# Hybrid decoder layer: the weight sums of the last feed-forward part are made in that part, and the factors of the dilated attention are worked out later

## The chip, the cores and the metric

The kernel runs on one core of a Trainium2 chip. The time is device time in microseconds (us) of one execution; "the time before" is the median of three runs. TensorE multiplies matrices, VectorE and ScalarE work on tiles in on-chip memory, POOL (GpSimd) does too and also issues transfers, and SP (SyncE) issues most transfers. Each engine runs its own instructions in order and waits for others by semaphores. "Granted clock" is the TensorE clock that the throttle granted, as a share of full speed.

## The reference, cut to what matters

```python
def swiglu(x, w_gate, w_up, w_down):
    return (jax.nn.silu(x @ w_gate) * (x @ w_up)) @ w_down

def dilated_attention(q, k, v):            # three groups (window, dilation), 4 heads each
    ...
    w = jax.nn.softmax(jnp.stack(lses), axis=0)            # over the groups
    o = jnp.sum(w[..., None] * jnp.stack(outs), axis=0)
    ...
def token_mixer(h, ...):
    ...                                     # proj = h @ w_in, split into q, k, v, gates, merge
    y_nsa = o_nsa.reshape(B, S, Q_NSA) @ w_nsa_o
    y_dil = o_dil.reshape(B, S, DIL_OUT) @ w_dil_o
    y = jax.nn.sigmoid(g_a) * y_nsa + jax.nn.sigmoid(g_b) * y_dil
    return y @ w_mix_out

def reference(x, ...):
    h = rms_norm(x, ffn1_pre)
    x = x + 0.5 * rms_norm(swiglu(h, ffn1 weights), ffn1_post)
    h = rms_norm(x, mix_pre)
    x = x + rms_norm(token_mixer(h, ...), mix_post)
    h = rms_norm(x, ffn2_pre)
    x = x + 0.5 * rms_norm(swiglu(h, ffn2 weights), ffn2_post)
    return x
```

x is 512 x 1024 in float32, the feed-forward width is 2816, and w_in is 1024 x 5656 (of it 2304 columns are q, k and v of the dilated attention and 2048 the two merge gates).

## The kernel before, in words

**Three parts in a row.** The first feed-forward part runs to about 320 us, the mixer (sparse attention, called nsa, then the dilated attention, called dil, then the output products) to about 790, and the last feed-forward part to the end.

**A float32 product is three matmuls.** Every operand is split into a rounded value (the cast on ScalarE, L162: tiles `whi`, and `x_s` where a slot named x holds it) and what is left (a subtraction on VectorE, L163: tiles `wlo`, or `SP_s`). Three matmuls (L185, L186, L187) multiply hi by hi, hi by lo and lo by hi into a bank of PSUM (`pb_F`, `pb_S`, `pb_V`, `pb_T`). So a weight comes by a transfer into a tile `raw`, is cast and subtracted, and only then can TensorE use it.

**The feed-forward parts work in pairs.** A part computes gate, up and their product for eleven pairs of feature blocks; `sums(p)` ends pair p and stores the odd half with a transfer of SP (L437, `odram`). The down product then uses seven block products, as in Strassen's method, and four of these need sums of blocks of the down weights. The sums are held in DRAM, `tdram` (four of them, td[0] to td[3]). The first load of a stored sum (L354, `raw<-tdram`) stands behind the last pair.

**Who makes these sums.** In the first part `weight_sums` makes them behind its own pairs, with 110 transfers of 256 KB through tiles `PT_s`. For the last part `table_sums` makes them: 32 transfers on POOL's queue from DRAM to DRAM, of 768 KB (24 of them) or 512 KB (8), four copies `wd` to `td` for each group of feature blocks (b = 0, 3, 6, 9; steps 0 and 1), then additions on top, by transfers that accumulate (step 2, then 5 and 8, or 4 and 6 for b = 9; each adds to, or reads, what an earlier one has written).

**Where the sums stand.** `after(name, src)` is a hook: where the table `SUMS_AT` has that name, POOL makes a copy of one element per partition from `src` (the mark, L1810) and issues the transfers of the table behind it. So the transfers can't start before `src` is there, and whatever POOL has behind the hook waits too. Before, the hooks stand all through the mixer: `rows`, `keys`, `gates`, `m2` to `m15` in nsa, `keys0`, `turn0` to `turn11`, `scaled1`, `scaled3` in dil, and `out0` to `out7` in the output products.

**The dilated attention's factors.** Each of the three groups leaves its maxima and sums of exponentials in a tile (`dst_t`). For groups 1 and 2, whose rows stand in another order, these go through DRAM (`sdram`, back as `nat_t`). The factors come from the minimum `mn` of the groups, three differences and exponentials `fac`, the sum `z`, its reciprocal and three products; two of them go through DRAM again (`fdram`, back as `gf_t`). POOL then scales all 12 x 4 tiles of probabilities (slots `PT_s`, `x_s`, `CP_s`, `CB_s`, L1673), and TensorE transposes the scaled tiles (L1722) and multiplies them with V. V is projected by a loop over pairs of weight blocks, `k0` = 0, 2, 4, 6, each of which casts and subtracts its weights (`wsplit`) and multiplies into four banks that VectorE reads (`Q_s`).

**The output products.** The merge gates were stored in `gdram` during the earlier work and come back as tiles (`SP_s<-gdram`) for the sigmoid. The end of nsa has its own weights, `in_nsa_w_cv` among them.

Transfers of the weights are issued by SP, in program order; a scheduler orders the instructions of every engine along the order in which the code is written, and `issue_after` adds an order between two of them.

Of the kernel before, what the change touches and what calls it, by code (L numbers as in the profile page):

```python
# [16 lines left out]
AF = mybir.ActivationFunctionType  # L17
OP = mybir.AluOpType
# [3 lines left out]
P = 128  # L22
# [3 lines left out]
NT = S // P  # L26
# [9 lines left out]
PLAN = (1, 2, 2, 5, 2, 2, 3, 5, 2, 1, 2, 1)  # L36
LOTS = (0, 2, 1, 3)
BLOCKS = ("P1", "P2", "P6", "P5", "P7", "P3", "P4")
SUMS_AT = dict(rows=[(0, 0), (0, 1)], keys=[(0, 2)], gates=[(0, 5)], m2=[(0, 8)],
               m14=[(3, 0)], m15=[(3, 1)], keys0=[(3, 2)], turn0=[(3, 5)], turn2=[(3, 8)],  # L40
               turn11=[(6, 0), (6, 1)], scaled1=[(6, 2)], scaled3=[(6, 5)], out0=[(6, 8), (9, 0)], out1=[(9, 1)], out3=[(9, 2)],
               out5=[(9, 4)], out7=[(9, 6)])
SUMMED = dict(P5=0, P6=1, P3=2, P7=3)
NSA_UNITS = 6
PLAIN_UNITS = 8
# [38 lines left out]
class Layer:  # L84
# [275 lines left out]
    def ffn(self, gu, wd, td, post, finish, xsrc, aside=None, opened=None):  # L360
# [3 lines left out]
        nc = self.nc  # L364
# [63 lines left out]
        def sums(p, ev, od):  # L428

            h = slice(0, 256), slice(256, 512)  # L430
            x, y = self.slot(X_TAGS[p] if opened else "CB" if p < KEEP else "PT"), self.slot("ring")
            nc.vector.tensor_sub(x[:, h[0]], ev[:, h[1]], od[:, h[1]])
            nc.vector.tensor_sub(x[:, h[1]], ev[:, h[0]], ev[:, h[1]])
            nc.vector.tensor_sub(ev[:, h[1]], x[:, h[0]], ev[:, h[0]])
            nc.vector.tensor_add(y[:, 0:256], od[:, h[0]], ev[:, h[1]])
            with self.tc.issue_after(self.last_refill):
                nc.sync.dma_start(self.odram[p], od)  # L437
                if opened or p < KEEP:
                    nc.sync.dma_start(self.sxdram[p], x)
                else:  # L440
                    kept[p] = x
                nc.sync.dma_start(self.ydram[p // 2][:, h[p % 2]], y[:, 0:256])
            E.append(ev)
            if opened:
                sums_behind(ev[:, 0:1], p + 1)

        def split_even(p):
            if p < later:
# [4 lines left out]
        def sums_behind(src, n):  # L453
            mark = self.sbt("mark", [P, 1])
            behind = nc.gpsimd.tensor_copy(mark, src).ins
            with self.tc.issue_after(behind):
                for q in SUMS[n]:
                    weight_sums(q)
# [56 lines left out]
        for m in range(len(t4)):  # L515
            n = 4 // len(t4)
            c = slice(m * n, m * n + n), slice(256, 512)
# [95 lines left out]
        for i, (p, name) in enumerate(todo):  # L613
# [6 lines left out]
            if p == NP - 1 and name in ("P4", "P3"):  # L620
                k0 = 2 * len(first)
                r = self.blocks_of.pop(("B11", k0))
# [605 lines left out]
    def nsa(self, fillers, sums):  # L1228
        nc = self.nc
        ident = lambda v: v  # L1230
        pe = self.positions()
        r = self.wcols([(C_KC, 256)])
# [13 lines left out]
            self.proj_T(None, b, (2 * P, S), w)  # L1246
        self.positions_T(pe)
        rows = [self.block_rows(b) for b, _ in early[:2]]
        self.after('rows', rows[1][1][:, 0:1])
        kw = early[3][0]  # L1250
        vw = self.v_weights()
        kparts = [self.k_parts(early[2][0], ident)]
        gs = [self.blocks(0, rows[0])]
        kparts.append(self.k_parts(kw, ident))
        self.after('keys', kparts[1][1][1][:, 0:1])
        gs.append(self.blocks(1, rows[1]))
        wq = self.wslots(self.wcols([(0, 64), (256, 64)]), ["Q", "Q", "of", "of"])
        self.v_nsa(vw)
        self.after('gates', self.gate[:, 3, 0:1])
        early = self.hidden_early(0)  # L1260
        self.oh, self.ol = [], []
        heads = [(i, half, br) for i in range(4) for half in range(2) for br in range(2)]
# [1 line left out]
        probs = {}  # L1264
        for n in range(len(heads) + LAG):
            if n < len(heads) and n % 4 == 0:
                i = n // 4
# [4 lines left out]
            m = n - LAG  # L1272
            if m >= 0:
                i, half, br = heads[m]
                with self.tc.issue_after(self.unit_mm) if m == 0 else ExitStack():
                    probs[m] = self.hb_probs(*live.pop(m), self.gate[:, :, (i + 4 * half) * 3 + 1 + br])
            if n < len(heads):
                i, half, br = heads[n]
# [6 lines left out]
            if m >= 0:  # L1285
                i, half, br = heads[m]
                with self.tc.issue_after(self.last_pool):
                    sums(m)
                if br == 0:
                    out = self.bank("V")  # L1290
# [196 lines left out]
    def dil(self, fillers, early_gates):  # L1487
        nc = self.nc
# [13 lines left out]
        stats, probs, raws, bias = [], [], {}, {}  # L1502
# [115 lines left out]
        pairs = {}  # L1618
# [4 lines left out]
        for j in range(2):  # L1623
            pairs[0, j] = project(0, j)
            self.load_blocks()
            self.after(f"keys{j}", pairs[0, j][0][1][:, 0:1])
            if j == 0:
                for name in ("T1", "T2", "T4", "T3"):
                    self.mix_token_sums((name,))
        for i, n in enumerate(PLAN):  # L1630
            (g, j), half = turns[i // 2], i % 2
            if (j, half) == (0, 0) and g:
                project(g, 0)
            attend(g, j, half)
            self.after(f"turn{i}", stats[g][:, 0, 2 * j + half, 0:1])
            blocks(n)

        nat = [stats[0]]
# [2 lines left out]
            nc.sync.dma_start(n_.rearrange("p t h s -> p t (h s)"), self.sdram[g].rearrange("(t p) c -> p t c", p=P))  # L1641
            nat.append(n_)
        mn = self.sbt("mn", [P, NT, 4])
        with self.tc.issue_after(self.last_sub):
            nc.vector.tensor_tensor(mn, nat[0][:, :, :, 0], nat[1][:, :, :, 0], op=OP.min)
        nc.vector.tensor_tensor(mn, mn, nat[2][:, :, :, 0], op=OP.min)
        fac = [self.sbt(f"fac{g}", [P, NT, 4]) for g in range(3)]
        z = self.sbt("z", [P, NT, 4])
        zt = self.sbt("zt", [P, NT, 4])
        for g in range(3):  # L1650
            nc.vector.tensor_sub(fac[g], mn, nat[g][:, :, :, 0])
            self.last_exp = nc.scalar.activation(fac[g], fac[g], AF.Exp).ins
            dst_ = z if g == 0 else zt
            nc.vector.scalar_tensor_tensor(dst_, nat[g][:, :, :, 1], 1e-30, fac[g], op0=OP.max, op1=OP.mult)
            if g:
                nc.vector.tensor_add(z, z, zt)
        nc.vector.reciprocal(z, z)
        gf = []
        for g in range(3):
            nc.vector.tensor_mul(fac[g], fac[g], z)  # L1660
            if g == 0:
                gf.append(fac[0])
            else:
                nc.sync.dma_start(self.fdram[g - 1].rearrange("(t p) c -> p t c", p=P), fac[g])
                f = self.sbt(f"gf{g}", [P, NT, 4])
                nc.sync.dma_start(f, self.fdram[g - 1].rearrange("(n r) c -> n r c", r=4))
                gf.append(f)

        for hh in range(4):
            for g in range(3):  # L1670
                for t in range(NT):
                    pr = probs[g][hh][t]
                    scaled = nc.gpsimd.tensor_scalar(pr, pr, gf[g][:, t, hh:hh + 1], None, op0=OP.mult).ins  # L1673
            with self.tc.issue_after(scaled):
                self.after(f'scaled{hh}')

        vt = []
        vtags = ["Q"] * 4 + ["KA"] * 4 + ["V"] * 4
# [8 lines left out]
        r = self.wcols([(C_VD, 256)])  # L1687
        ws = [self.wsplit(r[:, 4 * u:4 * u + 4], [4, 256]) for u in range(2)]
        vt.append([])
        for t in range(NT):  # L1690
            b = self.bank("FFVS"[t])
            c = slice(t * P, (t + 1) * P)
# [8 lines left out]
        for k0 in range(0, KT, 2):  # L1701
            if k0 % 4 == 0:
                r = self.raw(wv[:, k0:k0 + 4], [4, S])
            w = self.wsplit(r[:, k0 % 4:k0 % 4 + 2], [2, S])
            for j in range(2):
                xs = [x[k0 + j].rearrange("p (n r) -> p r n", r=4) for x in (self.xh, self.xl)]
                for t in range(NT):
                    self.mm3(banks[t], xs[0][:, t], xs[1][:, t], w[0][:, j], w[1][:, j], k0 + j == 0, k0 + j == KT - 1)
# [68 lines left out]
        for n in range(len(items) + 1):  # L1777
            if n < len(items):
                hh, g = items[n]
# [6 lines left out]
            hh, g = items[n - 1]  # L1786
# [5 lines left out]
            j, half = hh // 2, hh % 2  # L1792
# [9 lines left out]
    def after(self, name, src=None):  # L1802

        if name not in SUMS_AT:
            return
# [8 lines left out]
    def mixer(self, post, finish, sums):  # L1814
        nc, a, tc = self.nc, self.a, self.tc
# [23 lines left out]
        def early_sums(m):  # L1839
            self.lot_sums(0, m)  # L1840
            self.lot_sums(1, m - 5)
            self.after(f"m{m}")

        self.sums = sums
        self.nsa(fill_half, early_sums)
# [1 line left out]
        gates = [[None, None] for _ in range(KT)]  # L1847
# [44 lines left out]
        for d in range(KT):  # L1892
            if d % 4 == 0:
                rd = self.raw(wd[d // 4], [2, 512])
                w_d = self.wsplit(rd, [2, 512])
            if d % 2 == 0 and d >= EARLY:
                w = first_weights(d)
            b1, b2 = self.bank(), self.bank()
            if d >= EARLY:
                c = slice((d % 2) * P, (d % 2 + 1) * P)  # L1900
                for k in range(4):
                    self.mm3(b1, w[0][:, k, c], w[1][:, k, c], self.oh[k], self.ol[k], k == 0, k == 3)
            c = slice((d % 4) * P, (d % 4 + 1) * P)
            for k in range(2):
                self.mm3(b2, w_d[0][:, k, c], w_d[1][:, k, c], self.dh[k], self.dl[k], k == 0, k == 1)
            load_gates(d + GATES_AHEAD)
            g1, g2 = gates[d]
            for i, b in ((0, b1), (1, b2)):
                if i or d >= EARLY:
                    times(d, i, b, behind[d > 1])  # L1910
            nc.vector.tensor_add(g1, g1, g2)
            self.after(f'out{d}', g1[:, 0:1])
            hi, lo = self.slot(ytags[2 * d], F32R), self.slot(ytags[2 * d + 1], F32R)
            self.split(hi, lo, g1)
            ys.append((hi, lo))
# [201 lines left out]
```

## Time and profile before

| | |
|---|---|
| median of three runs | 1126.52 us (1125.6 to 1128.25) |
| profiled execution | 1127.78 us, of it the span 1125.9 us, granted clock 0.991 in the mean |
| TensorE busy | 1094.8 us (97%), 7166 matmuls |
| VectorE busy | 913.4 us (81%) |
| ScalarE busy | 665.9 us (59%) |
| POOL busy | 251.2 us (22%) |
| transfers | 250.65 MB, 223 GB/s in the mean; on POOL's queue 68.69 MB |

The span is what the profile's stretches and waits are measured in; the execution's own time has 1.9 us around it. Busy shares are means over the whole span. A wait is shown as "engine tile line <- engine tile line": the instruction that waited, and the one that ended its wait.

### The profile page before, as it was taken

Reading aid. Unit: us, or ns where it says so; the run is one execution under the profiler, and the core shown is the slowest. Engines: PE = TensorE matmul, PEld = TensorE weight load, DVE = VectorE, ACT = ScalarE, POOL = GpSimd, SP = SyncE. Lnnn points to the kernel's source line nnn. Section 1 sums busy time; section 2 is a strip of 40 time slices with the busy share of each in tenths; the row PEclk is TensorE's granted clock in tenths of the full one; section 3 lists DMA queues with packets and bytes.
Section 4 is the critical chain, followed back from the end, with each engine's and each line's share of the span. In section 5 each row is a group of like instructions: output and inputs, shape, how many; then the busy total and the mean of one; then the engine's idle time right before and its main releaser. Section 6 shows DMA issues by size and latency. Waiting matters only on the chain.

```text
span 1125.9 us, 19348 instructions
## 1 busy us (share of the span) xinstructions
PE 1094.8 (97%) x7166; PEld 987.5 (88%) x7166; DVE 913.4 (81%) x1569; ACT 665.9 (59%) x1202; POOL 251.2 (22%) x340
## 2 busy tenths in 40 slices
PE   9999999999999899999999999979999999999997
PEld 7899999987889787777999988867989999998885
DVE  6889999988787778787987547856888999989575
ACT  7455555566565678675887536635435555557452
POOL 0444454300021146453100068110000000000001
PEclk9999999999999999999999999989999999999999
DMA  9899999999864988866675747796324444479852
GB/s 353 240 277 327 303 283 297 286 338 329 281 201 156 278 278 235 236 166 200 157 224 180 263 126 180 220 300 222 113 97 143 137 133 135 121 230 295 283 183 100
DMA packets 88798, 250.65 MB, mean 223 GB/s; under 512 B 13024, under 2 KB 18176, under 8 KB 85760
## 3 DMA queue, kind: packets, MB, share of 16 engines
q1 hardware_dynamic: 68208, 180.44, 47.0%
q0 software_dynamic: 20064, 68.69, 24.3%
q8 instruction: 56, 0.92, 0.3%
q14 instruction: 38, 0.31, 0.1%
q10 hardware_dynamic: 432, 0.30, 0.1%
HBM read 214.73 MB, written 74.50 MB: 257 GB/s over the span
## 4 chain that ended last, share of the span: by engine, by line
PE 67%; DVE 13%; ACT 7%; DMA 7%; issue 3%; POOL 3%; SPq 0%; DVEq 0%; POOLq 0%; ACTq 0%
PE pb_S L187 6%; PE pb_F L187 6%; PE pb_F L186 6%; PE pb_F L185 6%; PE pb_S L185 6%; PE pb_S L186 6%; PE pb_T L187 5%; PE pb_T L185 5%; PE pb_T L186 5%; DVE wlo L163 3%; PE pb_V L185 2%; PE pb_V L186 2%; PE pb_V L187 2%; ACT whi L162 2%; POOL PT_s L1673 2%
## 5 line engine op out<-in xcount | busy, mean ns | idle before, releaser
L163 DVE TENSOR_TENSOR wlo<-raw,whi 128x1024 fp32r<-128x1024 f32 (+2 forms) x222 | 262.3, 1187 | 92.8 <-ACT whi L162 88.6
L162 ACT CAST whi<-raw 128x1024 fp32r<-128x1024 f32 (+2 forms) x222 | 225.8, 1019 | 125.7 <-PE pb_F L187 20.4
L185 PE MATMUL pb_F<-xhl_t,whi 128*128 128x256 f32 (+1 forms) x320 | 106.2, 332 | 0.3 <-DVE KA_s L930 0.2
L187 PE MATMUL pb_F<-xhl_t,wlo 128*128 128x256 f32 (+1 forms) x320 | 105.1, 328 | 0.0
L186 PE MATMUL pb_F<-xhl_t,whi 128*128 128x256 f32 (+1 forms) x320 | 104.9, 328 | 0.0
L206 POOL TENSOR_TENSOR rs_t<-rs_t,mhalf_t 128x1 f32<-128x1 f32 x20 | 13.3, 666 | 403.8 <-DVE rs_t L202 403.8
L185 PE MATMUL pb_S<-xhl_t,whi 128*128 128x256 f32 (+1 forms) x280 | 83.3, 297 | 0.0
L186 PE MATMUL pb_S<-xhl_t,whi 128*128 128x256 f32 (+1 forms) x280 | 83.1, 297 | 0.0
L187 PE MATMUL pb_S<-xhl_t,wlo 128*128 128x256 f32 (+1 forms) x280 | 83.1, 297 | 0.0
L185 PEld LDWEIGHTS pb_F<-xhl_t,whi 128*128 128x128 f32 x320 | 60.3, 188 | 5.7 <-issue 0.8
L187 PEld LDWEIGHTS pb_F<-xhl_t,wlo 128*128 128x128 f32 x320 | 60.2, 188 | 4.9 <-DVE wlo L163 0.3
L186 PEld LDWEIGHTS pb_F<-xhl_t,whi 128*128 128x128 f32 x320 | 60.3, 188 | 4.4 <-issue 0.2
L1193 POOL TENSOR_SCALAR SP_s<-SP_s,st_t 128x384 f32<-128x384 f32 (+2 forms) x48 | 48.9, 1050 | 58.7 <-ACT whi L162 17.3
L185 PE MATMUL pb_T<-xhl_t,whi 128*128 128x256 f32 x216 | 59.9, 277 | 0.0
L186 PE MATMUL pb_T<-xhl_t,whi 128*128 128x256 f32 x216 | 59.9, 277 | 0.0
L187 PE MATMUL pb_T<-xhl_t,wlo 128*128 128x256 f32 x216 | 59.9, 277 | 0.0
L186 PEld LDWEIGHTS pb_S<-xhl_t,whi 128*128 128x128 f32 x280 | 52.6, 188 | 2.2
L185 PEld LDWEIGHTS pb_S<-xhl_t,whi 128*128 128x128 f32 x280 | 52.6, 188 | 2.2
L187 PEld LDWEIGHTS pb_S<-xhl_t,wlo 128*128 128x128 f32 x280 | 52.6, 188 | 2.2
L162 ACT CAST whi<-tmp_t 128x1024 fp32r<-128x1024 f32 x36 | 36.4, 1051 | 30.4 <-DVE tmp_t L538 23.5
L185 PE MATMUL pb_T<-SP_s,whi 128*128 128x256 f32 x176 | 49.2, 279 | 1.6 <-ACT ring_s L1470 1.4
L187 PE MATMUL pb_T<-SP_s,wlo 128*128 128x256 f32 x176 | 49.0, 278 | 0.2 <-DVE wlo L163 0.2
(931 smaller groups left out, 3731.6 us busy)
## 6 DMA issues: line engine op xcount, KB each, us to landing
raw<-in_gu_dram SPq DMA_DIRECT2D x64, 512.0 KB, 5.3
raw<-tdram SPq DMA_DIRECT2D x40, 512.0 KB, 5.3
PT_s<-in_d_dram POOLq DMA_DIRECT2D x66, 256.0 KB, 6.9
raw<-in_d_dram SPq DMA_DIRECT2D x30, 512.0 KB, 4.6
tdram<-in_d_dram POOLq DMA_DIRECT2D x18, 768.0 KB, 12.0
ldram<-in_w_in_dram POOLq DMA_DIRECT2D x12, 1024.0 KB, 11.2
tdram<-PT_s POOLq DMA_DIRECT2D x44, 256.0 KB, 5.7
raw<-in_w_in_dram SPq DMA_DIRECT2D x11, 1024.0 KB, 5.5
```

Of the source, the lines that this page charges most:

```text
L162: self.last_cast = self.nc.scalar.copy(dsthi, src).ins
L163: self.last_sub = self.nc.vector.tensor_sub(dstlo, src, dsthi.bitcast(F32)).ins
L185: mm(out, lhi, rhi, start=start, stop=False, skip_group_check=skip)
L186: mm(out, lhi, rlo, start=False, stop=False, skip_group_check=skip)
L187: self.last_mm = mm(out, llo, rhi, start=False, stop=stop, skip_group_check=skip).ins
L206: nc.gpsimd.tensor_tensor(out=r, in0=v, in1=self.mhalf, op=OP.pow)
L1193: self.last_pool = nc.gpsimd.tensor_scalar(pp, pp, st[:, 1, t:t + 1], None, op0=OP.mult).ins
L1673: scaled = nc.gpsimd.tensor_scalar(pr, pr, gf[g][:, t, hh:hh + 1], None, op0=OP.mult).ins
```

## The change

1. `SUMS_AT` has eight names, `pair0` to `pair7`, and the hooks with these names stand in `sums(p)` of the last feed-forward part. All 32 sum transfers are now issued behind its first eight pairs, and all hooks in the mixer are gone.
2. In dil, the work from `mn` to POOL's scaling is a function, `factors()`, called in V's loop behind the weights of `k0 == 2` rather than ahead of the loop. The four transfers by `fdram` go to POOL's queue instead of SP's.

```diff
-SUMS_AT = dict(rows=[(0, 0), (0, 1)], keys=[(0, 2)], gates=[(0, 5)], m2=[(0, 8)],
-               m14=[(3, 0)], m15=[(3, 1)], keys0=[(3, 2)], turn0=[(3, 5)], turn2=[(3, 8)],
-               turn11=[(6, 0), (6, 1)], scaled1=[(6, 2)], scaled3=[(6, 5)], out0=[(6, 8), (9, 0)], out1=[(9, 1)], out3=[(9, 2)],
-               out5=[(9, 4)], out7=[(9, 6)])
+SUMS_AT = dict(pair0=[(0, 0), (0, 1)], pair1=[(3, 0), (3, 1)], pair2=[(0, 2), (3, 2), (6, 0)],
+               pair3=[(0, 5), (3, 5), (6, 1), (9, 0)], pair4=[(0, 8), (6, 2), (9, 1)], pair5=[(3, 8), (6, 5), (9, 2)],
+               pair6=[(6, 8), (9, 4)], pair7=[(9, 6)])
...
             if opened:
                 sums_behind(ev[:, 0:1], p + 1)
+            else:
+                self.after(f'pair{p}', ev[:, 0:1])
...
-        self.after('rows', rows[1][1][:, 0:1])
...
-        mn = self.sbt("mn", [P, NT, 4])
-        with self.tc.issue_after(self.last_sub):
-            nc.vector.tensor_tensor(mn, nat[0][:, :, :, 0], nat[1][:, :, :, 0], op=OP.min)
...
+        def factors():
+            with self.tc.issue_after(self.last_sub):
+                nc.vector.tensor_tensor(mn, nat[0][:, :, :, 0], nat[1][:, :, :, 0], op=OP.min)
...
-                nc.sync.dma_start(self.fdram[g - 1].rearrange("(t p) c -> p t c", p=P), fac[g])
+                    nc.gpsimd.dma_start(self.fdram[g - 1].rearrange("(t p) c -> p t c", p=P), fac[g])
...
-                nc.sync.dma_start(f, self.fdram[g - 1].rearrange("(n r) c -> n r c", r=4))
+                    nc.gpsimd.dma_start(f, self.fdram[g - 1].rearrange("(n r) c -> n r c", r=4))
...
-                    scaled = nc.gpsimd.tensor_scalar(pr, pr, gf[g][:, t, hh:hh + 1], None, op0=OP.mult).ins
-            with self.tc.issue_after(scaled):
-                self.after(f'scaled{hh}')
...
             w = self.wsplit(r[:, k0 % 4:k0 % 4 + 2], [2, S])
+            if k0 == 2:
+                factors()
...
-            self.after(f'out{d}', g1[:, 0:1])
```

The other hooks (`keys`, `gates`, `m`, `keys0` and `keys1`, `turn`) are taken out in the same way. The numbers of the lines shift by one to three in the changed kernel.

**POOL at the start of nsa.** The names: `rs_t` the norm's statistics, `mark_t` the marks, `tdram_95` the stored sums, `in_d_dram` the down weights of the last part, `dm_s` and `SP_s` distances and softmax pieces, `ldram` the tiles of another queue of weights. Before:

```order
L206 TENSOR_TENSOR rs_t<-rs_t,mhalf_t 128x1
L1810 COPY mark_t<-SP_s 128x1
L1316 DMA tdram_95<-in_d_dram 128x1536 x4
L1810 COPY mark_t<-KA_s 128x1
L1318 DMA tdram_95<-in_d_dram 128x1536
L1319 DMA tdram_95<-in_d_dram 128x1536
L1810 COPY mark_t<-gate_t 128x1
L1321 DMA tdram_95<-tdram_95 128x1536
L1493 AFFINE_SELECT of_s<-dm_s 128x256
L1193 TENSOR_SCALAR SP_s<-SP_s,st_t 128x384
```

Now:

```order
L205 TENSOR_TENSOR rs_t<-rs_t,mhalf_t 128x1
L1491 AFFINE_SELECT of_s<-dm_s 128x256
L1194 TENSOR_SCALAR SP_s<-SP_s,st_t 128x384
L1194 TENSOR_SCALAR SP_s<-SP_s,st_t 128x128
L1194 TENSOR_SCALAR SP_s<-SP_s,st_t 128x256
```

The three marks and seven sum transfers of this place have gone; POOL goes from the norm to the mask and the softmax pieces.

**VectorE around the factors.** Rows L951 (L952) read the scores of the last turn of attention; `Q_s` are V's banks, `wlo` V's and other weights, `SP_s` the residuals of the x slots. Before:

```order
L951 ISA dst_t 128x1
L163 TENSOR_TENSOR wlo<-raw,whi 128x1024
L1684 TENSOR_TENSOR Q_s<-pb_F,Q_s 128x4x64
L1646 TENSOR_TENSOR mn_t<-mn_t,nat_t 128x16
L1651 TENSOR_TENSOR fac_t<-mn_t,dst_t 128x16
L1651 TENSOR_TENSOR fac_t<-mn_t,nat_t 128x16 x2
L1654 SCALAR_TENSOR_TENSOR z_t<-dst_t,fac_t 128x16
L1654 SCALAR_TENSOR_TENSOR zt_t<-nat_t,fac_t 128x16
L1656 TENSOR_TENSOR z_t<-z_t,zt_t 128x16
```

Now:

```order
L162 TENSOR_TENSOR wlo<-raw,whi 128x1024
L1680 TENSOR_TENSOR Q_s<-pb_F,Q_s 128x4x64 x2
L1680 TENSOR_TENSOR Q_s<-pb_V,Q_s 128x4x64
L162 TENSOR_TENSOR wlo<-raw,whi 128x1024
L1680 TENSOR_TENSOR Q_s<-pb_S,Q_s 128x4x64
L1642 TENSOR_TENSOR mn_t<-dst_t,nat_t 128x16
L162 TENSOR_TENSOR wlo<-raw,whi 128x1024
L1643 TENSOR_TENSOR mn_t<-mn_t,nat_t 128x16
L162 TENSOR_TENSOR SP_s<-x_s 128x512
L1648 TENSOR_TENSOR fac_t<-mn_t,dst_t 128x16
L1648 TENSOR_TENSOR fac_t<-mn_t,nat_t 128x16 x2
```

The factors stand behind all four banks of V's first two weight blocks and the weights of the next, and residuals of weights and of x slots stand between their pieces.

**POOL from the scaling to the last part.** The probabilities (`PT_s`, `x_s`, `CP_s`, `CB_s`) are scaled, then, before, the sums of the output products follow:

```order
L1673 TENSOR_SCALAR x_s<-x_s,gf_t 128x128 x5
L1673 TENSOR_SCALAR CP_s<-CP_s,gf_t 128x128 x4
L1673 TENSOR_SCALAR x_s<-x_s,gf_t 128x128 x3
L1673 TENSOR_SCALAR CP_s<-CP_s,gf_t 128x128 x4
L1318 DMA tdram_95<-in_d_dram 128x1536
L1319 DMA tdram_95<-in_d_dram 128x1536
L1673 TENSOR_SCALAR x_s<-x_s,gf_t 128x128 x4
L1673 TENSOR_SCALAR CP_s<-CP_s,gf_t 128x128 x8
L1673 TENSOR_SCALAR CB_s<-CB_s,gf_t 128x128 x4
L1321 DMA tdram_95<-tdram_95 128x1536
L1810 COPY mark_t<-KB_s 128x1
L1323 DMA tdram_95<-tdram_95 128x1536
```

Now:

```order
L1670 TENSOR_SCALAR PT_s<-PT_s,fac_t 128x128
L1661 DMA fdram<-fac_t 128x4x4 x2
L1670 TENSOR_SCALAR PT_s<-PT_s,fac_t 128x256 x3
L1670 TENSOR_SCALAR PT_s<-PT_s,fac_t 128x128
L1670 TENSOR_SCALAR PT_s<-PT_s,fac_t 128x256 x3
L1663 DMA gf_t<-fdram 128x16 x2
L1670 TENSOR_SCALAR PT_s<-PT_s,fac_t 128x128
L1670 TENSOR_SCALAR PT_s<-PT_s,fac_t 128x256 x3
L1670 TENSOR_SCALAR PT_s<-PT_s,fac_t 128x128
L1670 TENSOR_SCALAR PT_s<-PT_s,fac_t 128x256 x3
L1670 TENSOR_SCALAR x_s<-x_s,gf_t 128x128 x4
```

The sums are gone from between and behind the scaling, and the factors' transfers stand among its first pieces.

More of the change, by code (lines that the diff above doesn't have):

```diff
@@ L1254, in nsa @@
         kparts.append(self.k_parts(kw, ident))
-        self.after('keys', kparts[1][1][1][:, 0:1])
         gs.append(self.blocks(1, rows[1]))
@@ L1258, in nsa @@
         self.v_nsa(vw)
-        self.after('gates', self.gate[:, 3, 0:1])
         early = self.hidden_early(0)
@@ L1625, in dil @@
             self.load_blocks()
-            self.after(f"keys{j}", pairs[0, j][0][1][:, 0:1])
             if j == 0:
@@ L1634, in dil @@
             attend(g, j, half)
-            self.after(f"turn{i}", stats[g][:, 0, 2 * j + half, 0:1])
             blocks(n)
@@ L1643, in dil @@
         mn = self.sbt("mn", [P, NT, 4])
-        with self.tc.issue_after(self.last_sub):
-            nc.vector.tensor_tensor(mn, nat[0][:, :, :, 0], nat[1][:, :, :, 0], op=OP.min)
[L1646 to L1663, printed above, removed]
-                nc.sync.dma_start(self.fdram[g - 1].rearrange("(t p) c -> p t c", p=P), fac[g])
-                f = self.sbt(f"gf{g}", [P, NT, 4])
-                nc.sync.dma_start(f, self.fdram[g - 1].rearrange("(n r) c -> n r c", r=4))
-                gf.append(f)
-        for hh in range(4):
-            for g in range(3):
-                for t in range(NT):
-                    pr = probs[g][hh][t]
-                    scaled = nc.gpsimd.tensor_scalar(pr, pr, gf[g][:, t, hh:hh + 1], None, op0=OP.mult).ins
-            with self.tc.issue_after(scaled):
-                self.after(f'scaled{hh}')
+        def factors():
+            with self.tc.issue_after(self.last_sub):
+                nc.vector.tensor_tensor(mn, nat[0][:, :, :, 0], nat[1][:, :, :, 0], op=OP.min)
+            nc.vector.tensor_tensor(mn, mn, nat[2][:, :, :, 0], op=OP.min)
+            fac = [self.sbt(f"fac{g}", [P, NT, 4]) for g in range(3)]
+            z = self.sbt("z", [P, NT, 4])
+            zt = self.sbt("zt", [P, NT, 4])
+            for g in range(3):
+                nc.vector.tensor_sub(fac[g], mn, nat[g][:, :, :, 0])
+                self.last_exp = nc.scalar.activation(fac[g], fac[g], AF.Exp).ins
+                dst_ = z if g == 0 else zt
+                nc.vector.scalar_tensor_tensor(dst_, nat[g][:, :, :, 1], 1e-30, fac[g], op0=OP.max, op1=OP.mult)
+                if g:
+                    nc.vector.tensor_add(z, z, zt)
+            nc.vector.reciprocal(z, z)
+            gf = []
+            for g in range(3):
+                nc.vector.tensor_mul(fac[g], fac[g], z)
+                if g == 0:
+                    gf.append(fac[0])
+                else:
+                    nc.gpsimd.dma_start(self.fdram[g - 1].rearrange("(t p) c -> p t c", p=P), fac[g])
+                    f = self.sbt(f"gf{g}", [P, NT, 4])
+                    nc.gpsimd.dma_start(f, self.fdram[g - 1].rearrange("(n r) c -> n r c", r=4))
+                    gf.append(f)
+            for hh in range(4):
+                for g in range(3):
+                    for t in range(NT):
+                        pr = probs[g][hh][t]
+                        nc.gpsimd.tensor_scalar(pr, pr, gf[g][:, t, hh:hh + 1], None, op0=OP.mult)
@@ L1841, in early_sums @@
             self.lot_sums(1, m - 5)
-            self.after(f"m{m}")
         self.sums = sums
```

## The prediction

> **What bounds the kernel.** I read the page first (busy shares, the 40 slices), then the waits of TensorE by stretch, then the table by stretches, and last the chain of waits around each hole. The page:
>
> ```profile
> span 1125.9 us, 19348 instructions
> DMA  9899999999864988866675747796324444479852
> ```
>
> TensorE is busy 1094.8 us of this span, so only some 31 us are to be had, and the question is in which holes they lie and what ends them. Three waits of the mixer, the longest it has there, carry the case (line waiting, what ended it, us in total, times, longest):
>
> ```profile
> PE pb_V L1039 <- ACT x_s L162: 4.7, 1, 4.7
> PE pb_S L185 <- ACT whi L162: 1.4, 1, 1.4
> PE pb_S L186 <- DVE wlo L163: 1.2, 1, 1.2
> PE pb_S L187 <- DVE wlo L163: 6.3, 1, 6.3
> ```
>
> In the table by stretches the last three columns are granted clock, DMA share and GB/s:
>
> ```profile
> 386.00:392.00 6.00, 1.39 (x5) 1.22 (x6) 3.03 (x7) 5.28 (x13) 0.00 (x0) 0.81 0.84 251
> 392.00:398.00 6.00, 6.00 (x31) 5.69 (x30) 4.49 (x14) 4.32 (x14) 1.42 (x2) 0.62 0.66 187
> 655.00:660.00 5.00, 2.43 (x7) 1.73 (x7) 4.65 (x16) 3.54 (x9) 3.29 (x3) 0.94 0.10 3
> 660.00:665.00 5.00, 5.00 (x17) 4.35 (x17) 3.40 (x6) 2.71 (x4) 5.00 (x4) 0.72 0.43 108
> 736.00:740.00 4.00, 0.00 (x0) 0.00 (x0) 2.27 (x3) 1.27 (x3) 0.84 (x1) 0.74 1.04 405
> 740.00:744.00 4.00, 3.79 (x9) 3.01 (x10) 2.18 (x5) 2.48 (x4) 1.04 (x2) 0.50 1.04 251
> ```
>
> Each hole is paid twice: the idle time, and then a lower clock on the work behind it. The second price is 0.38 x 6 = 2.3 us behind hole A (386), 0.28 x 5 + 0.06 x 5 = 1.7 behind B (655) and 0.50 x 4 = 2.0 behind C (736). A costs 4.7 + 2.3 = 7.0, B 2.6 + 1.7 = 4.3, C 6.3 + 2.0 = 8.3: together 19.6 us. The chain shows that a transfer ends each:
>
> ```profile
> 376.45 10.25 DMA raw<-in_nsa_w_cv_dram
> 640.07 8.95 DMA sdram<-dst_t
> 649.08 5.30 DMA nat_t<-sdram
> 726.31 10.23 DMA SP_s<-gdram
> ```
>
> In the 40 slices those places stand at a DMA share of 0.7 to 0.9, while the last part's pairs (844 to 985) stand at 0.4: there is room where the sums go.
>
> **The change, part by part.** 1. *The 32 sum transfers leave the mixer.* 24 of 768 KB and 8 of 512 KB, 22 MB. In A, seven of them run while the load is under way; the same kinds of load have these medians, under contention and over all:
>
> ```profile
> tdram<-in_d_dram POOLq DMA_DIRECT2D x6, 768.0 KB, 12.7
> raw<-in_w_in_dram SPq DMA_DIRECT2D x11, 1024.0 KB, 5.5
> SP_s<-gdram SPq DMA_DIRECT2D x12, 256.0 KB, 5.4
> KB_s<-gdram SPq DMA_DIRECT2D x4, 256.0 KB, 4.9
> ```
>
> A: with 5.5 us the load issued at 376.45 lands at 382.0 instead of 386.7, 4.7 earlier. ScalarE's queue behind it (a cast, eight pieces of softmax, the cast TensorE waits for, 3.7 us in all) moves along, but it also has casts of its own that end at 382.2, so I take 4.3 of the idle 4.7:
>
> ```profile
> 381.02 1.14 ACT L162 CAST x_s<-raw 128x512 fp32r<-128x512 f32 x2 [2.41 <-PE pb_S L946]
> ```
>
> Of the clock price I take half, 1.2, since the weight casts behind stay in ScalarE's pace. Bounds: 0 (the load is slow for its own sake) and 7.0.
>
> C: with 4.9 us the load issued at 726.31 lands at 731.2, 5.3 earlier, and all behind it up to the weight residual that TensorE waits for moves along. Of the idle 6.3 us 1.0 stays. A pause that small cost no clock elsewhere (8.64 busy of 10 us, in one wait, at 1.00):
>
> ```profile
> 570.00:580.00 10.00, 8.64 (x74) 8.44 (x73) 8.33 (x19) 9.45 (x19) 0.12 (x1) 1.00 0.62 223
> ```
>
> So 5.3 + 2.0 = 7.3. Bounds 2 and 8.3: five sum transfers (2.75 MB) are issued from 724.5, but twelve gate tiles and two weight tiles remain.
>
> The Trainium skill (DMA: Bandwidth & Descriptors, Anatomy of one DMA) fits a transfer as about 2 us plus its bytes at 436 GB/s; by it A's 1 MB would take an estimated 4.4 us and C's 256 KB an estimated 2.6, and the sum would be about 1.5 us better. The medians above are longer, as transfers here always overlap others, so they stand.
>
> 2. *The factors.* VectorE stands still for 11.4 us, in its own order, for the statistics' way through DRAM, with the residuals of V behind it:
>
> ```profile
> 654.48 0.18 DVE L1646 TENSOR_TENSOR mn_t<-mn_t,nat_t 128x16 f32<-128x16 f32 x1 [11.40 <-DMA nat_t<-sdram]
> 656.72 19.84 POOL L1673 TENSOR_SCALAR PT_s<-PT_s,fac_t 128x128 f32<-128x128 f32 x16 [15.68 <-DVE fac_t L1660]
> 676.53 3.79 POOL L1673 TENSOR_SCALAR x_s<-x_s,gf_t 128x128 f32<-128x128 f32 x5
> 638.96 2.08 POOL L1316 DMA_DIRECT2D tdram<-in_d_dram  x4 [0.29 <-issue]
> 684.04 0.44 PE pb_T L1722 x4
> ```
>
> Now the residuals of V's first two weight tiles stand ahead, so B goes whole: 4.3 us. But VectorE reaches the factors only behind the fourth V bank (about 650) and a residual, and three more residuals are mixed in (0.7 us each): last factor at about 656.5, where it was. The earlier landing (three 768 KB copies no longer beside it) thus buys nothing, and POOL starts its scaling at the same 656.7. POOL now also issues the factors' four transfers, taken from SP: 2.08 / 4 = 0.52 us each, 2.1 us before the group-1 tiles (bounds 0 and 4.4, at the 1.1 of the slowest copy issue). Their first four were ready at 676.53 + 3.79 x 4 / 5 = 679.6 and will be at 681.7. TensorE's transposes of them were at 684.04, could be at 679.7 and must now wait 2.0 us. So 4.3 - 2.0 = 2.3, less a new clock price of up to 1.7: I take 0.6, the lower end, as the two waits of B (2.6 us together) did cost clock. Bounds +4.3 and -1.7. SP loses four entries, which nothing waited behind.
>
> The Trainium skill (TensorE: Matmul & The Clock Gate, Why this matters for your kernels) asks only that idle gaps stay under about 3 us. By it a 2.0 us wait costs no clock and B gives 2.3, the sum 1.7 us better; B's rows, 0.72 behind 2.6 us of idle in two pieces, do not bear it out, so the lower end stays.
>
> 3. *The sums in the last part.* Its pairs must carry 22 MB more. The first part is the model: it makes the same sums behind its pairs with 110 transfers of 256 KB (27.5 MB). One stretch of each (TensorE, its loads, VectorE, ScalarE, POOL, clock, DMA), and their weight loads (count, KB, median landing):
>
> ```profile
> 110.00:120.00 10.00, 10.00 (x91) 10.00 (x90) 10.00 (x17) 5.82 (x9) 4.32 (x6) 1.00 1.01 260
> 900.00:910.00 10.00, 10.00 (x91) 10.00 (x90) 9.81 (x15) 6.80 (x9) 0.00 (x0) 1.00 0.48 128
> raw<-in_gu_dram SPq DMA_DIRECT2D x13, 512.0 KB, 6.0
> raw<-in_gu_dram SPq DMA_DIRECT2D x15, 512.0 KB, 3.9
> 113.95 0.50 SPq L437 DMA_DIRECT2D odram<-W_s  x1
> 132.99 0.49 SPq L437 DMA_DIRECT2D odram<-W_s  x1
> 901.49 0.43 SPq L437 DMA_DIRECT2D odram<-W_s  x1
> 920.53 0.42 SPq L437 DMA_DIRECT2D odram<-W_s  x1
> ```
>
> A pair takes 19.04 us in both, at DMA shares 1.01 and 0.48, and TensorE issues 91 matmuls in 10 us in both. So the sums cost nothing there; the cover is the ring of eight weight blocks, two pairs deep, so that a load has some 25 us where it needs 6. Bounds 0 and 2 us. The dates hold too:
>
> ```profile
> 958.62 0.43 SPq L437 DMA_DIRECT2D odram<-W_s  x1
> 1012.36 1.75 SPq L354 DMA_DIRECT2D raw<-tdram  x2
> ```
>
> The last sum is issued behind pair 7 (about 960) and lands some 13 us later; the first load of a sum is at 1012. Eight mark copies on POOL cost nothing: it has no other work between the norms and the end.
>
> *Sum:* A 4.3 + 1.2, B 0.6, C 5.3 + 2.0, last part 0: 13.4 us. Span 1125.9 - 13.4 = 1112.5. The profiled execution took 1127.78 with 1.9 around its span: 1114.4. The median of the runs shown is 1126.52, 1.26 below it, so I predict 1126.5 - 13.4 = 1113.1.
>
> **The rivals.**
> *R1, POOL is in time:* its scaling goes faster once VectorE is less busy beside it, and B keeps its 4.3. For: five tiles took 6.78 us at first and 5.89 later:
>
> ```profile
> 656.72 6.78 POOL PT_s L1673 x5
> 663.84 5.89 POOL PT_s L1673 x5
> ```
>
> Against: the four issues. 13.4 + 3.7 = 17.1, so 1109.4.
> *R2, the loads stay slow:* in A, three 1 MB weight loads are themselves under way at 376, in C twelve gate tiles and two weight tiles. The shares around A stay near 1.0 for 25 us, and half of it is SP's own 5.1 MB against 5.5 MB of POOL's. Half of A and C: 13.4 - 6.4 = 7.0, so 1119.5.
> *R3, slower: POOL falls behind the pairs.* Its queue is in order, and a sum waits for the landing of the copy under it. Pairs 2 to 6 hold two dependent landings each; at 13 us that is 26 us in a 19-us pair, 7 us lost per pair, 35 by pair 6. The mark copy that reads a pair's result then holds a ring tile, three of them, which VectorE needs two pairs on. It decides once a mark is over 19 us late; by 35 - 19 = 16 us, paid in full and with clock 2.0 behind it: 1113.1 + 18 = 1131. For: in the first part POOL was already some 10 us behind its pair (result stored at 113.95, mark at 123.73):
>
> ```profile
> 123.73 0.55 POOL L455 COPY mark_t<-KB_s 128x1 f32<-128x1 f32 x1
> ```
>
> Against: there it stayed 10 behind for eight pairs, and here the copy under a sum is one pair older.
> *R4, POOL is kept from issuing while VectorE works.* With only VectorE's idle 0.2 us of 10 (900 to 910), six issues of 0.52 us could not be made in a pair, the sums would still be under way at 1012, and every late us would stand on the path: 1140 or more. Against: at 110 to 120 VectorE is busy 10.00 and POOL issues all the same (4.32 us). The Trainium skill (SBUF — State Buffer, the 'DVE blocks DMA' trap) has this rule, for VectorE instructions that take both ports; the trace does not bear it out for the subtractions here.
> *R5, no change:* each hole reopens at the next late engine; 1126.5.
>
> **How the numbers follow.** Forecast 0.58, R1 0.14, R2 0.16, R3 0.05, R4 0.02, R5 0.05. A measurement of this kernel tells about 0.2% (2.3 us) from no change. Faster: 0.58 + 0.14 + 0.16 = 0.88; same 0.05; slower 0.07. The range reaches over R1's 1109.4, with B and C at their better ends, to 1108.0, and over R2's 1119.5 to 1120.5; outside lie R3 to R5 (0.12) and the rims.
>
> **What would show it.** Right: the clock row at 1.00 through the stretches of A and C; the load behind 376 landing in under 7 us and the gate tile in under 6; VectorE's 11.4 us wait gone, but POOL's scaling starting where it did and TensorE's transposes waiting for POOL by 1 to 3 us; pairs of the last part at 19.0 us with a DMA share near 0.8 to 0.9. Wrong: pairs longer than 19.3 us or SP waiting for a sum at the first load (R3, R4), A or C with over 3 us idle (R2), no wait for POOL (R1).

## The result, and the profile after

The changed kernel takes 1114.53 us (median of four runs, 1113.68 to 1115.58) against 1126.06 before (four runs, 1123.16 to 1128.25). The ratio is 0.990 with a 95% interval of 0.9875 to 0.9924, clear of 1: it is faster by 11.5 us. 1113.1 was forecast. The profiled execution took 1113.99. Its page:

```profile
span 1112.2 us, 19346 instructions
...
PE   9999999999999999999999999999999989999997
DMA  9899999999863478863265623673589997468862
```

The slices of TensorE at holes A and C (8 and 7 before) are 9 now, and there is a new 8 in the 33rd slice, in the last part, where transfers now stand at 9. The longest waits of TensorE between 320 and 800 us, then the only long one behind 800:

```profile
PE pb_T L184 <- ACT ring_s L1468: 1.4, 1, 1.4
PE pb_S L186 <- DVE wlo L162: 1.1, 1, 1.1
```
```profile
PE pb_T L184 <- ACT V_s L577: 3.9, 1, 3.9
```

The waits of A, B and C are gone (the 1.4 for `ring_s` was there before). The stretches that answer to those of before (A, B, C), and the new hole D:

```profile
386.00:392.00 6.00, 5.90 (x36) 5.01 (x36) 5.87 (x19) 5.92 (x16) 1.62 (x2) 1.00 0.70 209
655.00:660.00 5.00, 5.00 (x23) 5.00 (x22) 1.02 (x1) 0.67 (x1) 4.98 (x7) 1.00 0.13 35
736.00:740.00 4.00, 4.00 (x19) 3.34 (x18) 3.10 (x5) 2.94 (x6) 0.00 (x0) 1.00 0.90 328
886.00:890.00 4.00, 3.22 (x29) 3.02 (x27) 3.13 (x5) 1.57 (x2) 0.00 (x0) 1.00 1.03 242
890.00:893.00 3.00, 0.00 (x0) 0.00 (x0) 0.38 (x2) 0.82 (x3) 0.00 (x0) 1.00 1.02 406
893.00:897.00 4.00, 3.88 (x21) 3.88 (x22) 3.01 (x4) 1.02 (x2) 3.78 (x5) 0.63 1.03 415
```

TensorE is busy at clock 1.00 where the three holes were; at 890 it has nothing to do, then a clock of 0.63.

TensorE's instructions stand in the same order in both kernels, so the start of one and the same matmul in both traces shows where time was won. "Ahead by" is how much earlier that matmul starts now, and "step" what has been won since the row above. Worked out from the traces' matmul rows (us):

```
matmul behind       before     after    ahead by    step
(first part)        273.82    273.17      0.65
hole A              396.51    388.62      7.89     A  +7.2
(turns of dil)      626.20    618.82      7.38        -0.5
hole B              662.70    650.44     12.27     B  +4.9
hole C              744.92    725.50     19.43     C  +7.2
(norms)             786.65    767.01     19.64        +0.2
hole D              911.00    897.23     13.77     D  -5.9
end                1119.37   1105.41     13.96        +0.2
```

The profiled executions differ by 13.8 us (1127.78 and 1113.99); the one of before lies 1.7 above its median, the one of the changed kernel 0.5 below. The steps are thus those of two single executions, and they add up to more than the 11.5 us between the medians.

What ends D is seen in the chain of waits, and in the rows of ScalarE and POOL:

```profile
868.99 23.11 DMA ydram<-ring_s
```
```profile
892.18 0.42 ACT L424 ACTIVATE ring_s<-V_s 128x256 f32<-128x256 f32 x1 [4.13 <-DMA ydram<-ring_s]
893.18 0.52 POOL L1808 COPY mark_t<-ring_s 128x1 f32<-128x1 f32 x1 [18.37 <-DVE ring_s L425]
```

A pair's result y is stored from a slot of the ring `ring` (three slots). One store of 128 KB took 23.11 us. ScalarE needed that slot for its next product and stood still for 4.13 us, and with it, in its queue, the copy that empties TensorE's bank (`V_s`). POOL was not late: it had waited 18.37 us for the mark's source.

### The profile page after: what moved, and what is told of

Same layout as the page of the kernel before. It is cut to its first block, busy times and chain, and to the rows that moved or that the text cites. A ratio compares the mean times of both kernels' runs of the same rounds, so it can differ in the third digit from the quotient of the medians.

```text
span 1112.2 us, 19346 instructions
## 1 busy us (share of the span) xinstructions
PE 1090.3 (98%) x7166; PEld 984.8 (89%) x7166; DVE 913.1 (82%) x1569; ACT 666.5 (60%) x1202; POOL 236.6 (21%) x340
## 5 line engine op out<-in xcount | busy, mean ns | idle before, releaser
L205 POOL TENSOR_TENSOR rs_t<-rs_t,mhalf_t 128x1 f32<-128x1 f32 x20 | 13.5, 673 | 306.2 <-DVE rs_t L201 306.2
```

The source lines that it names most:

```text
L205: nc.gpsimd.tensor_tensor(out=r, in0=v, in1=self.mhalf, op=OP.pow)
```

## The experiments

Each was run in turn with the kernel before on one chip, and ratios are to that: E1 to E4 on one chip, E5 to E8 on a second, E9 to E11 on a third.

**E1, the sums alone.**

```diff
-            if k0 == 2:
-                factors()          # and mn ... scaling inline ahead of V's loop, fdram and gf on SP, as before
```

> The changed kernel with the factors put back ahead of V's loop and their transfers back on SP; the sums stay in the last part. Theory 1 (hole B came from the three sum copies beside the statistics' way through DRAM, so moving the sums alone closes it): the statistics land about 10 us sooner on this clockwork, VectorE waits under 4 us for them, TensorE has no wait over 1 us at that place, time as the changed kernel, 1114.5 (1113 to 1116). Theory 2 (it is the later place of the factors that closes B): the hole is back with 4.9 us, 1119.4 (1118 to 1121).

1114.83 us against 1124.24, ratio 0.9913 (0.9899 to 0.9928). No wait of TensorE over 1.4 us is left in the mixer, and VectorE's wait for the statistics is short:

```profile
DVE mn_t L1642 <- DMA nat_t<-sdram: 3.0, 1, 3.0
```

Theory 1: without the copies beside them the statistics come in time. D is there, with 4.4 us.

**E2, the factors alone.** The kernel before with `factors()` at `k0 == 2` and its transfers on POOL; all sums and hooks of the mixer stay.

> The kernel before with the later factors and their transfers on POOL, all sums left in the mixer. Holes A and C must stay (7 us each) and the new hole of the last part at 890 must not be there. Theory 1 (the sums alone make B): VectorE still waits for the statistics until about 654 and the residuals behind them are late, 1125 to 1126. Theory 2 (the later place closes B by itself): 1126.1 - 4.9 = 1121.2 (1120 to 1122.5). If both this and the sums alone close B, the two parts cover the same hole and are not to be added.

1121.01 us, ratio 0.9967 (0.9955 to 0.998): 3.2 us less. The waits of TensorE between 360 and 760:

```profile
PE pb_S L187 <- DVE wlo L163: 6.8, 1, 6.8
PE pb_V L1039 <- ACT x_s L162: 5.5, 1, 5.5
```

A and C stay, B is closed (a step of 4.9 us in the matmuls' starts, between the rows at 626.20 and 662.70 of before), D is absent. Theory 1's form for this run is wrong: the later place closes B by itself too. The time lies in theory 2's range, but that was worked out from 1126.1; from this chip's 1124.24, 4.9 us less would be 1119.3, and the medians show 3.2.

**E3, the sums spread; and E4, slots of their own for y.** E3:

```diff
-SUMS_AT = dict(pair0=[(0, 0), (0, 1)], pair1=[(3, 0), (3, 1)], pair2=[(0, 2), (3, 2), (6, 0)], ...
+SUMS_AT = dict(pair0=[(0, 0), (0, 1)], pair1=[(0, 2), (3, 0)], pair2=[(3, 1), (0, 5)],
+               pair3=[(3, 2), (0, 8)], pair4=[(6, 0), (3, 5)], pair5=[(6, 1), (3, 8)],
+               pair6=[(6, 2), (9, 0)], pair7=[(9, 1), (6, 5)], pair8=[(9, 2), (6, 8)], pair9=[(9, 4), (9, 6)])
```

> The changed kernel with the same 32 sum transfers spread over ten pairs, three or four behind each, instead of 4, 4, 6, 6, 5, 4, 2, 1. Theory P (the new hole of 5.4 us at 890 comes from too many sum transfers in flight behind pairs 2 to 4, which stretch a store to 23 us): the wait of 3.9 us is gone, no store of the part takes over 12 us, 1114.5 - 5.4 = 1109.1 (1108 to 1111). Theory Q (22 MB in this part cost what they cost wherever they stand): 1114.5, with a wait of the same size at another pair.

E4:

```diff
-            ..., self.slot("ring")
+            ..., self.slot("ring" if opened else {4: "PT", 5: "CB"}.get(p, "ring"))
```

> The changed kernel with the y tiles of pairs 4 and 5 in slots of their own instead of the ring of three; all transfers as they are. Theory R (the hole at 890 is a ring slot held by the slow store of y, on which ScalarE's next product waits): the 3.9 us wait goes though the transfers stay as slow as 20 us, 1109 to 1110.5. Theory W (with landings of 20 us the weights of the pairs are late too): the wait only changes its name to a weight tile, 1113 to 1115.

E3: 1106.85 us, ratio 0.9842 (0.9827 to 0.9856). E4: 1110.41 us, ratio 0.9878 (0.9859 to 0.9897). The landings of the y stores (least, median, most), of the changed kernel, E3 and E4:

```profile
DMA to landing us min/median/max: 2.8/4.9/23.1
```
```profile
DMA to landing us min/median/max: 3.6/4.0/7.0
```
```profile
DMA to landing us min/median/max: 3.2/6.0/25.2
```

E4 leaves the stores as slow as they were, and the 3.9 us wait is gone: the slot was the link (theory R). E3 leaves the slots and takes the slowness: gone as well (P). E3 gains more than its range said (1108 to 1111), of which 1.8 us are this chip's faster kernel before (1124.24, not 1126.06). E4 stays 3.6 us behind E3; waits for weights that land late, theory W's, are 1.4 of these:

```profile
PE pb_F L186 <- DVE wlo L162: 0.9, 1, 0.9
PE pb_S L186 <- DVE wlo L162: 0.5, 1, 0.5
```

**E5, E6, E7: one hole's transfers each, in the kernel before.** E5 moves `rows`, `keys`, `gates` and `m2` to pairs 0 to 3; E6 issues the copies of `turn11` behind `turn6`; E7 moves `out0` to `out7` to pairs 0 to 4. E5 moves 4, 2, 1 and 1 transfers to its four pairs, and E7 nine (eight are counted in what was expected of it).

> The kernel before with only the sums of the first group (seven of their eight transfers are under way around 386) moved to pairs 0 to 3, two to four transfers in a pair. Theory 1 (hole A is the sum transfers beside the load of the last nsa weights): the load lands in under 6 us, A closes, 7.0 us less than before (6 to 8), B and C stay, and no new hole in the last part. Theory 2 (SP's own loads slow each other there, rival R2): half, 3 to 4 us less.

> The kernel before with only the four copies that stand beside the statistics' way through DRAM issued earlier, behind turn 6 instead of turn 11; factors as before. Theory 1 (these copies make hole B): the statistics' two transfers take under 7 us instead of 14, VectorE waits under 4 us, B closes, 4 to 5 us less than before. Theory 2 (B is VectorE's order, whatever the copies): no change within 1 us. A and C stay in both.

> The kernel before with only the eight sum transfers of the output products moved to pairs 0 to 4, one to three in a pair. Theory 1 (hole C is these transfers beside the merge gates' tiles): the gate tile lands in under 6 us, C closes, 7.0 us less than before (6 to 8), A and B stay. Theory 2 (the twelve gate tiles and two weight tiles slow each other, rival R2): half, 3 to 4 us less.

E5: 1119.58 against 1124.53, ratio 0.9957 (0.994 to 0.9974). The two loads issued between 374 and 378 (the nsa weights and a projection's weights), before and in E5:

```profile
DMA to landing us min/median/max: 10.3/12.4/14.6
```
```profile
DMA to landing us min/median/max: 5.4/6.0/6.6
```

A closes (6.7 us in the matmuls' starts, between those at 273.82 and 396.51 of before); C stays, as two waits of 2.6 and 3.8 us. The median says 5.0 us less, which lies between the ranges of the two theories; the load, 5.4 us in place of 10.3, is what speaks for theory 1.

E6: 1122.56, ratio 0.9976 (0.9967 to 0.9985): 2.0 us by the medians (2.7 by the ratio), in neither theory's range, though the matmuls' starts say 4.8 at B. The profiled execution of before is 3.3 above this chip's median, so its holes may be larger than most executions have; that was not settled. The mechanism is in the trace: VectorE's wait at the statistics, 11.40 before, and no wait of TensorE at that place:

```profile
DVE mn_t L1646 <- DMA nat_t<-sdram: 2.8, 1, 2.8
```

E7: 1118.06, ratio 0.9938 (0.9925 to 0.9951), 6.5 us less. The stretches of C:

```profile
736.00:740.00 4.00, 4.00 (x19) 3.27 (x18) 4.00 (x6) 0.77 (x1) 0.00 (x0) 1.00 0.95 297
740.00:744.00 4.00, 4.00 (x19) 3.30 (x18) 2.28 (x4) 1.94 (x4) 0.00 (x0) 1.00 1.04 359
```

The twelve gate tiles are still there; the slowest lands in 5.8 us, where it was 11.1 before (before, then E7):

```profile
DMA to landing us min/median/max: 3.3/5.4/11.1
```
```profile
DMA to landing us min/median/max: 2.7/5.1/5.8
```

TensorE's wait at this place is 1.1 us in place of 6.3. Rival R2, by which SP's own loads slow each other, falls in A and in C: each load is fast once the sums are gone.

**E8, spread sums with the factors as before.**

> All sums spread over ten pairs as in the earlier run, and the factors back ahead of V's loop with their transfers on SP. If the two edits cover the same hole, the factors' place is worth nothing once no sum stands in the mixer: the time of the spread kernel, a ratio to the kernel before of 0.984 (0.983 to 0.986). If the later place has a worth of its own: 2 to 5 us more, 0.986 to 0.989.

1107.81, ratio 0.985 (0.9838 to 0.9863), beside 0.9842 (0.9827 to 0.9856) for E3: no difference that these runs can tell. Once no sum stands in the mixer, the later factors are worth nothing measurable.

E8 takes out all three holes at once. By the matmuls' starts the sum is nearly the same either way: 6.7 + 4.8 + 7.2 = 18.7 in E5, E6 and E7, and 19.2 in E8. The medians do not: 5.0 + 2.0 + 6.5 = 13.5, but 16.7 for E8 (1124.53 less 1107.81). So the sizes of A, B and C by the traces are those of one execution of before; how large they are in most executions these runs leave open, by some 3 us in their sum.

**E9, E10, E11: how much a pair can carry, on one chip.** E9:

```diff
+SUMS_AT = dict(pair0=[(0, 0), (0, 1)], pair1=[(3, 0), (3, 1)], pair2=[(0, 2), (3, 2)],
+               pair3=[(6, 0), (6, 1)], pair4=[(0, 5), (3, 5), (9, 0)], pair5=[(6, 2), (9, 1)],
+               pair6=[(0, 8), (3, 8), (9, 2)], pair7=[(6, 5), (9, 4), (6, 8), (9, 6)])
```

> The changed kernel with the sums behind the same eight pairs, but four transfers behind every one (2.5 to 3.0 MB) instead of up to six (4.5 MB). Theory P as a rate: with the last part saturated it moved 301 GB/s, and SP's own 129 GB/s leave 172 GB/s, that is 3.3 MB in a pair of 19.04 us. Four transfers stay just under it: no backlog carries over, no store over 14 us, the 3.9 us wait is gone, ratio to the kernel before 0.984 to 0.987. If it is the number of pairs that counts (22 MB in 150 us is too much whatever the order), the hole comes back at pair 3 to 6, 0.988 to 0.991.

> The changed kernel unaltered, so that the others of this call stand beside it on one chip. Theory: ratio 0.990 (0.988 to 0.992) to the kernel before and the wait of 3.9 to 4.4 us at 890 in its profile. If it is over 0.993 or the wait is missing, the new hole is not a property of the kernel, and the gains of the spread kernels would be read wrongly.

> The kernel with the sums spread over ten pairs, three or four transfers behind each, unaltered, beside the changed kernel on one chip. Theory: 7 us less than the changed kernel (6 to 8.5), ratio to the kernel before 0.984. Of these 7, 5.4 to 6 are the hole at 890; the rest must be smaller waits. If it is under 5, the two earlier medians came from different chips and not from the kernels.

E9: 1107.81, ratio 0.9843 (0.9822 to 0.9865). E10, the changed kernel: 1115.19, 0.9911 (0.9891 to 0.9932), and its wait is there with 3.8 us. E11, as E3: 1108.15, 0.9855 (0.983 to 0.9879). The transfers between 835 and 915, in the kernel before, the changed one, E9 and E3:

```profile
DMA packets 3752, 10.33 MB, mean 129 GB/s; under 512 B 416, under 2 KB 928, under 8 KB 3744
```
```profile
DMA packets 6284, 24.10 MB, mean 301 GB/s; under 512 B 699, under 2 KB 1083, under 8 KB 6276
raw<-in_gu_dram SPq DMA_DIRECT2D x13, 512.0 KB, 15.0
```
```profile
DMA packets 6111, 22.42 MB, mean 280 GB/s; under 512 B 672, under 2 KB 1184, under 8 KB 6103
raw<-in_gu_dram SPq DMA_DIRECT2D x13, 512.0 KB, 8.7
```
```profile
DMA packets 5450, 19.88 MB, mean 248 GB/s; under 512 B 601, under 2 KB 1113, under 8 KB 5441
raw<-in_gu_dram SPq DMA_DIRECT2D x13, 512.0 KB, 6.7
```

The changed kernel moved 301 GB/s over these 80 us with its transfer engines full all the time, and a weight took 15.0 us. It asks for more: behind pair 2, SP's 129 GB/s x 19.04 us = 2.5 million bytes and six sums of 768 KB, 4.7 million, are 7.2 million in a pair, 376 GB/s. What isn't moved in a pair is carried into the next. E9 has the same 22 MB in the same eight pairs, never over four behind one, and no wait; its slowest y store took 9.6 us:

```profile
DMA to landing us min/median/max: 2.8/3.9/9.6
```

So it is what is asked for behind one pair that opens D, not the sum of the bytes and not the number of pairs. Of the 7.0 us between E10 and E11, some 5.9 are D, and more in executions with the slower matmuls told of at the end.

The 301 GB/s is what this mix came to, and not a fixed limit: within these 80 us the slices of the profile go from 206 to 432 GB/s with the engines full. The first part, between 100 and 190, moves nearly as much, with full engines too, and its y stores are fast:

```profile
DMA packets 10336, 26.75 MB, mean 297 GB/s; under 512 B 1360, under 2 KB 2000, under 8 KB 10327
DMA to landing us min/median/max: 3.9/5.0/8.6
119.82 0.56 POOL L412 DMA_DIRECT2D tdram<-PT_s  x1 [2.46 <-DMA PT_s<-in_d_dram]
```

There POOL waits for landings before it issues more (2.46 us in this row), so few of its transfers are under way at a time. In the last part POOL issues up to six transfers at once. Whether the demand over a whole pair or the burst makes the backlog is not told apart: E3 and E9 lower both.

## Why the prediction was right, and where only its sum was

The time came within the range. The account is right in three places (A, C, and that B's hole closes) and wrong in two (what B pays for it, and the last part), with opposite signs.

- **A, 5.5 forecast, 7.2 in the trace.** Mechanism right (E5). The load went out 1.0 us earlier and took 5.1 us, not the 5.5 taken; the whole idle time and the whole clock price went, not 4.3 and half of 2.3. ScalarE's other casts, which were to keep 0.4 of it, left TensorE a wait of 0.2.
- **B, 0.6 forecast, 4.9 in the trace.** The factors are where the prediction put them: the scaling's start is 7.76 us earlier than before and A's lead is 7.4. The step that failed is "their first four were ready at 679.6 and will be at 681.7", and with it the 2.0 us wait for POOL. It took POOL's pace as fixed. (The 679.6 is a mean over five tiles; the fourth ended at 678.9.) POOL's rows now:

```profile
648.96 0.61 POOL L1670 TENSOR_SCALAR PT_s<-PT_s,fac_t 128x128 f32<-128x128 f32 x1 [53.30 <-DVE fac_t L1657]
651.17 6.55 POOL L1670 TENSOR_SCALAR PT_s<-PT_s,fac_t 128x256 f32<-128x256 f32 x7
658.86 7.13 POOL L1670 TENSOR_SCALAR PT_s<-PT_s,fac_t 128x128 f32<-128x128 f32 x8
665.98 3.34 POOL L1670 TENSOR_SCALAR x_s<-x_s,gf_t 128x128 f32<-128x128 f32 x4
```

  The sixteen PT tiles take 14.3 us, 0.89 each, where they took 19.84 (1.24 each); the four issues add 2.8 (2.1 was forecast). The x tiles are ready at 669.3, on the clock of before 676.7 instead of 681.7; TensorE's transposes of them begin at 671.7, and no wait for POOL is over 0.5 us. That is rival R1's mechanism, to which the prediction gave 0.14: POOL goes faster where VectorE is less busy beside it (1.02 of the 5 us from 655 now, 4.65 before). The trace of before shows it tile by tile. Five tiles from 657.3 to 663.8, with VectorE busy 5.40 of the 7 us from 657, and three from 669.7, where it is busy 0.00 of 2.60:

```profile
L1673 POOL TENSOR_SCALAR PT_s<-PT_s,fac_t x5: 1107/1982/2395, 657.3 to 663.8; 128x256 f32<-128x256 f32 x4, 128x128 f32<-128x128 f32 x1
L1673 POOL TENSOR_SCALAR PT_s<-PT_s,fac_t x3: 921/922/922, 669.7 to 671.5; 128x256 f32<-128x256 f32 x3
```

  A tile of 128x256 takes 0.92 to 0.96 us in both kernels when no subtraction (`wlo`, `SP_s`) of VectorE runs beside it. In before seven of the sixteen take over 1.1 us, and all seven have such a subtraction beside them; in the changed kernel only two are slowed, to 1.44 and 1.45. (R1's own rows, 6.78 and 5.89 for five tiles, are pieces of the chain of waits; from start to start the fives took 7.1 and 6.7 and the last six 6.0.) Nor is the factors' place what it was taken for: the transfers alone close B (E1, E6), the place alone closes it (E2), and with the transfers gone the place adds nothing (E8). "The earlier landing thus buys nothing" holds only with the later place. And one reading of the slices was wrong for B: the slice with 655 in it stands at a DMA share of 0.4, the one before it at 0.7.
- **C, 7.3 forecast, 7.2 in the trace**, by the mechanism told (E7): 1.1 us of the wait stay, where 1.0 was said.
- **The last part, 0 forecast (bounds 0 and 2), -5.9 in the trace.** The step that failed is "the first part is the model". It compared 22 MB with 27.5 MB, as totals. In the same count the first part has 2.5 MB behind each of eleven pairs, issued as earlier ones land; here up to 4.5 MB are issued at once behind one. And its cover, "the ring of eight weight blocks", is the weights' cover: weights of 15 to 20 us did no harm that can be seen in the changed kernel's waits. The three slots of `ring`, which a store must leave first, were not looked at. R3 had the backlog, pair by pair, but put it into POOL's queue and on the mark; it was in the transfers, and the mark's copy was never late. The prediction's own signs say the same: a DMA share of 0.8 to 0.9 was to be right for these pairs, and from 835 to 915 it is 1.03 to 1.05; pairs over 19.3 us were to be wrong, and the pair with D is 5.9 longer.

The traces' steps add up to 7.2 + 4.9 + 7.2 - 5.9 = 13.4, just the forecast's sum: the B term short by 4.3 and A by 1.7 paid for the 5.9. That is luck, and by the medians the sum is 11.5, not 13.4. A measured time alone would have confirmed all four terms.

Three rules can be held against the rows. The Trainium skill (SBUF — State Buffer, SBUF: two separate sides) says that a VectorE instruction with two inputs in SBUF and a POOL instruction that reads SBUF exclude each other for their whole length. The trace agrees: a 128x256 tile of POOL took 0.92 us with VectorE idle and up to 2.40 beside VectorE's subtractions of two SBUF tiles. The Trainium skill (DMA: Bandwidth & Descriptors, Issuing engines are not separate DMA queues) says that transfers started by different engines run on the same 16 DMA engines and interleave. The trace agrees: SP's store took 23.11 us behind POOL's sums. And the Trainium skill (TensorE: Matmul & The Clock Gate, Why this matters for your kernels) warns only of gaps over about 3 us; here B's two waits of 2.6 us together gave 4.9 back, so their clock price was real.

**A version that beats both:** spreading the sums to at most four behind a pair takes 0.984 to 0.986 of the kernel before (E3, E9, E11), and 7.0 and 7.4 us less than the changed kernel on the same chip (E11, E9).

## What to carry to other kernels

Moving background transfers to a quiet stretch is priced by what is asked for there, stretch by stretch, against what the transfer engines were seen to move with that mix, and not by the total; and the cover to check is the shortest ring among all that wait for a landing, stores included. Two edits that close the same hole are not to be added: price each with the other already made. A predicted total that comes out right says little about its terms; the starts of the same matmul in both traces show each term by itself.

## What was not expected of the hardware

In two of the three profiles that have hole D (E1 and E10), TensorE ran slower long after it. The stretch 930 to 950 in the changed kernel's first profile and in E10:

```profile
930.00:950.00 20.00, 20.00 (x179) 20.00 (x178) 18.93 (x25) 11.30 (x17) 1.29 (x2) 1.00 0.57 153
```
```profile
930.00:950.00 20.00, 20.00 (x172) 20.00 (x171) 18.23 (x24) 10.67 (x15) 1.29 (x2) 1.00 0.57 152
```

172 matmuls instead of 179 in 20 us, from the hole to about 990, some 4 us in all, at a granted clock of 1.00 in both. These executions were the slowest of their kernels (1117.0 and 1118.13 us). In the other profiles the same slow pace (118 ns from one such matmul to the next, not 113) comes for 20 us or less, at 210, 800 or 980 to 1000, that of before among them; only behind D did it last for 90. What sets it is open; no run was made on it.
